# Two linear scans of a hybrid transformer block on one core: 64-token chunks in two passes, or centred 128-token chunks with the states first

## The chip, the core and the metric

The kernel runs on one core of a Trainium2 chip. A core has a matrix engine (TensorE, PE), a vector engine (VectorE, DVE), an activation engine (ScalarE, ACT), a general-purpose engine (GpSimd, POOL) and an engine that issues most transfers here (SyncE, SP). Each takes its instructions in the order in which they were laid down and waits on semaphores. Matmuls read SBUF and write PSUM, which has eight banks of 128 partitions x 512 fp32 values. The metric is device time in microseconds, the median over runs.

## The reference

Two layers work on 256 context tokens and 1024 latent tokens of width 1024. Each layer normalises and modulates its input, projects it (`w_in`), feeds four mixers (a convolution, a gated linear attention, a softmax attention and a retention), projects their outputs and adds an MLP. The second layer needs no outputs for the context. The part that is changed is the linear scan of the gated attention and of the retention, four heads each, keys of 32 and values of 64, forward and backward:

```
b = cumsum(log_a within a chunk)
q_dec = q * exp(b);  k_inv = k * exp(-b);  k_end = k * exp(b_last - b)
scores = where(lower_tri, q_dec @ k_inv.T, 0);  o_intra = scores @ v
kv = k_end.T @ v;  S = exp(b_last) * S + kv      # chunk after chunk
o = o_intra + q_dec @ S_before
```

Context and latents are one sequence of 1280 tokens; backward, the context is scanned first too. The two directions' outputs are added, normalised per head (`rms_norm`), scaled and gated. In the gated attention the decay `log_a` differs per token and key channel and comes from a small projection `z`; in the retention it is one constant per head, and queries and keys of the latents are rotated.

## The kernel before

The tokens stand in three blocks, `t` = 0, 1, 2, of 256, 512 and 512 tokens, or ten tiles `i` of 128. All large products are exact to nearly fp32 by splitting both sides in a high and a low part (`whi`/`wlo`, `ahi`/`alo`) and summing three matmuls of reduced fp32 (`mm3`); `colA` gives channels x tokens, `tokB` tokens x channels. Small products are fp32, and a trace shows each as two passes.

A layer goes through stages: convolution inputs and gates, attention operands, the gated attention's projection (`gla_in`), the retention's (`ret_in`, with the end of the convolution, `conv_tail`, beside it), then the mixers, the output projection and the MLP. Between projection and mixers the operands go through DRAM (`glaraw`, `retraw`, `attraw`).

*Projection.* `gla_in` projects one tile with two `tokB` of 264 columns. From `z` it makes `la`, the log of the decay (`gab`), with one matmul and four elementwise steps, four cumulated sums with the 64-token matrices `tri`, their exponentials (`gex`), and six products (`gpre`). `ret_in` projects 512 columns and rotates token-major.

*Mixers.* Pass 1 (`gla1`, `ret1`) loads a tile, forms outer products of keys and values, steps the forward state, transposes queries and keys, spreads the queries over four heads (`gqef`, `gqeb`, `rqe`), forms scores, masks them, and makes forward outputs and the backward direction's inner part. Then `gla_states` and `ret_states` run the backward states, and pass 2 (`gla2`, `ret2`) adds the backward state's part and finishes a tile (`finish`: norm, two transposes, gate). A gated tile is two chunks of 64 tokens, a retention tile one of 128.

The attention runs beside this, one step of `attend` for each step of the scans, in three streams: `prep` (transposes of queries and keys into a bank, from there two ScalarE copies `ka`, and `kb`, `qa`), `rowmax` (scores of a tile against all keys, three segments of 512, 512 and 256, each reduced by VectorE), and `main` (scores `sb`, exponential `aP`, weights times values `ob`, running sums). The two heads of a `main` step write the two halves of one bank `ob`. What is left of it when the scans end runs alone.

PSUM in the mixers: `sb` 2 banks, `ob` 1, `mb` 1, `pb` 1, `gb` 2, `rb` 1. `prep` uses `pb`, and `rowmax` alternates:

```
b = bank(("mb", "pb")[(h_ + j) % 2])
```

The order on each engine is that of a scheduling layer, which starts from the program's order and moves instructions past each other by its own estimates; the tables of order below show what came out.

Of the kernel before, what the change touches and what calls it, by code (L numbers as in the profile page):

```python
# [8 lines left out]
F32 = mybir.dt.float32  # L9
# [22 lines left out]
def _consts():  # L32
# [3 lines left out]
    same = (p[:, None] // 64) == (p[None, :] // 64)  # L36
    s, t = p[:, None], p[None, :]
    sl, tl = (p % 64)[:, None], np.arange(64)[None, :]
    parts["maskfb"] = np.concatenate([(sl <= tl) * 1.0, (sl >= tl) * 1.0], axis=1)
    parts["tri"] = np.concatenate(  # L40
        [(same & (s <= t)) / 16.0, (same & (s > t)) / 16.0, (same & (s >= t)) / 16.0, (same & (s < t)) / 16.0], axis=1)
    parts["ind"] = np.stack([(p < 64) / 16.0, (p >= 64) / 16.0], axis=1)
    lg = np.log1p(-np.exp2(-5.0 - np.arange(4)))
# [4 lines left out]
    blk = (p[:, None] // 32 == np.arange(4)[None, :]) * 1.0  # L48
    parts["blk"] = blk * sc
    parts["retqf"] = (blk[:, :, None] * np.exp((t + 1) * hp)[:, None, :]).reshape(128, 512)  # L50
    parts["retqb"] = (blk[:, :, None] * np.exp((128 - t) * hp)[:, None, :]).reshape(128, 512)
# [3 lines left out]
    for nm, hd in (("ret", 32), ("att", 64)):  # L55
        n = hd // 4
        inv = 10000.0 ** (-np.arange(n) / n)
        ang = np.concatenate([(tok // 64)[..., None] * inv, (tok % 64)[..., None] * inv], axis=-1)
        parts["cos" + nm] = np.cos(ang).reshape(128, -1)
        parts["sin" + nm] = np.sin(ang).reshape(128, -1)  # L60
# [33 lines left out]
def build(tc, a, out, dbg=None):  # L94
# [41 lines left out]
    retraw = dram.tile([NTILE, 128, 512], F32, name="retraw")  # L136
    glaraw = dram.tile([NTILE, 128, 1024], F32, name="glaraw")
# [222 lines left out]
    # ------------------------------------------------------------------ start  # L360
# [53 lines left out]
    for l in range(2):  # L414
# [3 lines left out]
        # -------------------------------------------------------- in projections  # L418
# [15 lines left out]

        def raw():
            return ag.tile([128, 528], F32, tag="rst", name="rst", bufs=5)
# [82 lines left out]
        # attention operands: rms norm and rotation, token-major  # L519
# [70 lines left out]
        # gated linear attention operands: decays, decayed queries and keys  # L590
        ag = pools.get("ag", bufs=2)
        tri = ag.tile([128, 512], F32, name="tri", bufs=1)
        ind = ag.tile([128, 2], F32, name="ind", bufs=1)
        nc.sync.dma_start(out=tri, in_=cslice("tri"))
        nc.sync.dma_start(out=ind, in_=cslice("ind"))
        sl = granule(l, [(C_GLA, 512), (C_GLAZ, 16)], 528)

        def gla_in(i):
            need_o = not (last and i < CT)
            st = raw()  # L600
            b = tokB(sl, 264, 264, i)
            nc.scalar.copy(st[:, 264:528], b[:, 0:264])
            b = tokB(sl, 0, 264, i)
            nc.scalar.copy(st[:, 0:264], b[:, 0:264])
            q, k, z = st[:, 0:128], st[:, 128:256], st[:, 512:528]
            nc.sync.dma_start(out=glaraw[i, :, 768:1024], in_=st[:, 256:512])
            zt = ag.tile([17, 128], F32, tag="zt", name="zt")
            nc.gpsimd.memset(zt, 1.0)
            yield
            b = bank(f"c{i % 2}")  # L610
            tr(b[0:16, 256:384], z)
# [3 lines left out]
            ab = ag.tile([128, 256], F32, tag="gab", name="gab")  # L615
            nc.scalar.activation(ab, b[:, 0:256], AF.Abs)
            act(ab, ab, AF.Exp, "exp", scale=-1.0)
            act(ab, ab, AF.Ln, "exp", bias=1.0)
            la = ab
            nc.vector.scalar_tensor_tensor(la, b[:, 0:256], 0.0, ab, op0=ALU.min, op1=ALU.subtract)  # L620
# [4 lines left out]
            b = bank(f"c{i % 2}")  # L625
            for j in range(4):
                mm(b[:, j * 128:(j + 1) * 128], tri[:, j * 128:(j + 1) * 128], la[:, (j // 2) * 128:(j // 2) * 128 + 128], True, True)
            yield
            pre = ag.tile([128, 6, 128], F32, tag="gpre", name="gpre")
            ex = ag.tile([128, 4, 128], F32, tag="gex", name="gex")  # L630
            act(ex.rearrange("p a b -> p (a b)"), b, AF.Exp, "exp")
            if need_o:
                act(pre[:, 2:4, :], b.rearrange("p (a b) -> p a b", a=4)[:, 0:4:2, :], AF.Exp, "exp", scale=-1.0)
            yield
            kb_ = k[:, None, :].to_broadcast([128, 2, 128])
            nc.vector.tensor_tensor(pre[:, 4:6, :], ex[:, 1:4:2, :], kb_, op=ALU.mult)
            if need_o:
                nc.vector.tensor_tensor(pre[:, 0:2, :], ex[:, 0:4:2, :], q[:, None, :].to_broadcast([128, 2, 128]), op=ALU.mult)
                nc.vector.tensor_tensor(pre[:, 2:4, :], pre[:, 2:4, :], kb_, op=ALU.mult)
            x0 = 0 if need_o else 512  # L640
            nc.sync.dma_start(out=glaraw[i, :, x0:768], in_=pre.rearrange("p a b -> p (a b)")[:, x0:768])

        for _ in stagger((gla_in(i) for i in range(NTILE)), 1):
            step(taps, 3)
            step(mg)
        drain(taps)
        pools.close("ag")
        open_xy()

        ar = pools.get("ar", side="right", bufs=2)  # L650
        cosr = ar.tile([128, 8, 16], F32, name="cosr", bufs=1)
        sinr = ar.tile([128, 8, 16], F32, name="sinr", bufs=1)
        nc.sync.dma_start(out=cosr.rearrange("p a b -> p (a b)"), in_=cslice("cosret"))
        nc.sync.dma_start(out=sinr.rearrange("p a b -> p (a b)"), in_=cslice("sinret"))
        sl = granule(l, [(C_RET, 512)], 512)
        pw = load_slab(a["conv_w_pw"][l].rearrange("(k p) n -> p k n", p=128), 2, 256)
        y = [None if last and t == 0 else xy_tile(t, "y") for t in range(3)]

        def ret_in(i):
            st = ar.tile([128, 512], F32, tag="rst", name="rst")  # L660
            c0 = 128 if last and i < CT else 0
            b = tokB(sl, c0, 512 - c0, i)
            nc.scalar.copy(st[:, c0:512], b[:, 0:512 - c0])
            yield
            if i >= CT:
                t1 = ar.tile([128, 16, 16], F32, tag="rt1", name="rt1", bufs=1)
                t2 = ar.tile([128, 16, 16], F32, tag="rt2", name="rt2", bufs=1)
                x3 = st[:, 0:256].rearrange("p (h d) -> p h d", d=16)
                j = i - CT
                nc.gpsimd.tensor_tensor(t2, x3, sinr[:, j:j + 1, :].to_broadcast([128, 16, 16]), op=ALU.mult)  # L670
# [576 lines left out]
```

## Time and profile before

| | |
|---|---|
| median of 3 runs | 3361.87 us (3356.07 to 3367.40) |
| span of the profiled execution | 3332.9 us |
| its own time outside the span | not recorded; the median is 29.0 us above the span |
| PE busy | 3248.3 us (97%), 17209 matmul passes |
| DVE, ACT, POOL busy | 1762.8, 920.1, 245.8 us |
| granted clock, mean | 0.962 (1 is 2.4 GHz, 0.50 is 1.2 GHz) |
| gated projection, layer 0 | 268 to 352 us |
| retention projection, layer 0 | 352 to 425.5 us |
| mixers, layer 0 | 425.5 to 776 us |
| mixers, layer 1 | 2139.2 to 2500 us |

Busy time of PE counts a matmul until its modelled end, so neighbours overlap; how far apart two matmuls start says more than how long one takes. The clock is listed for each stretch. L numbers are lines of the kernel before; all matmuls have the helper's line L166, transposes L163.

### The profile page before, as it was taken

What the parts mean: (1) busy time and instruction counts of PE and PEld (TensorE: products, weight loads), DVE (VectorE), ACT (ScalarE), POOL (GpSimd) and SP (SyncE); (2) the same over time, 40 slices, a digit from 0 to 9 for tenths busy, and PEclk for the clock granted to TensorE, in tenths of its full rate; (3) what the DMA queues carried; (4) which work ended last, traced back from release to release, by engine and by line L of the source; (5) the groups of instructions that cost most, each with busy time, mean ns of one, the idle gap of its engine ahead of it and who ended that gap; (6) DMA issues with size and microseconds to landing.
All of it is one profiled execution on the core that took longest, in us unless ns stands there. A gap on an engine that the chain in (4) does not pass through costs nothing. (4 is left out here: it accounts for less than half of the span.)

```text
span 3332.9 us, 42190 instructions
## 1 busy us (share of the span) xinstructions
PE 3248.3 (97%) x17209; PEld 2475.9 (74%) x17209; DVE 1762.8 (53%) x3026; ACT 920.1 (28%) x1839; POOL 245.8 (7%) x255
## 2 busy tenths in 40 slices
PE   7999989999999999999999999899999999999999
PEld 5778856556888888888888779666557788888887
DVE  4683344676554444454446892235674644444545
ACT  4123432334322111111113334322243311111222
POOL 0011110331000000000000020201340000000000
PEclk8999997999999999999999999858899999999999
DMA  8354131003122222211111222210003111111111
GB/s 277 94 161 133 62 109 35 14 17 117 37 91 83 89 83 76 89 51 39 39 38 59 87 82 79 73 60 29 4 29 120 57 40 43 51 51 51 51 38 51
DMA packets 206523, 232.26 MB, mean 70 GB/s; under 512 B 19714, under 2 KB 160728, under 8 KB 206328
## 3 DMA queue, kind: packets, MB, share of 16 engines
q1 hardware_dynamic: 205592, 227.84, 21.4%
q8 instruction: 135, 2.21, 0.3%
q0 software_dynamic: 736, 1.72, 0.2%
q14 instruction: 60, 0.49, 0.0%
HBM read 191.11 MB, written 38.40 MB: 69 GB/s over the span
## 5 line engine op out<-in xcount | busy, mean ns | idle before, releaser
L166 PE MATMUL bank<-ahi,whi 128*128 128x512 f32 (+1 forms) x1920 | 720.0, 375 | 13.5 <-ACT tmp L153 6.6
L166 PE MATMUL bank<-ahi,wlo 128*128 128x512 f32 (+1 forms) x1920 | 720.5, 375 | 0.0
L166 PE MATMUL bank<-alo,whi 128*128 128x512 f32 (+1 forms) x1920 | 719.6, 375 | 0.9 <-DVE alo L357 0.9
L1156 DVE SCALAR_TENSOR_TENSOR x<-bank,mods,x 128x512 f32<-128x512 f32 (+1 forms) x640 | 438.5, 694 | 260.7 <-PE bank L166 259.0
L166 PE MATMUL bank<-hh,whi 128*128 128x512 f32 (+1 forms) x1280 | 475.9, 372 | 0.0
L166 PE MATMUL bank<-hl,whi 128*128 128x512 f32 (+1 forms) x1280 | 475.3, 371 | 0.0
L166 PE MATMUL bank<-hh,wlo 128*128 128x512 f32 (+1 forms) x1280 | 473.9, 370 | 0.0
L166 PEld LDWEIGHTS bank<-ahi,whi 128*128 128x128 f32 x1920 | 364.8, 190 | 100.5 <-DVE x L1156 8.2
L166 PEld LDWEIGHTS bank<-alo,whi 128*128 128x128 f32 x1920 | 362.9, 189 | 73.3 <-DVE alo L357 2.0
L166 PEld LDWEIGHTS bank<-ahi,wlo 128*128 128x128 f32 x1920 | 362.2, 189 | 67.8 <-issue 2.1
L160 DVE TENSOR_TENSOR wlo<-wst,whi 128x1024 fp32r<-128x1024 f32 (+1 forms) x186 | 224.9, 1223 | 269.1 <-ACT whi L159 268.9
L159 ACT CAST whi<-wst 128x1024 fp32r<-128x1024 f32 (+1 forms) x186 | 191.6, 1044 | 621.6 <-PE bank L166 473.1
L166 PEld LDWEIGHTS bank<-hh,whi 128*128 128x128 f32 x1280 | 240.5, 188 | 45.6
L166 PEld LDWEIGHTS bank<-hh,wlo 128*128 128x128 f32 x1280 | 239.9, 187 | 46.5 <-issue 0.2
L166 PEld LDWEIGHTS bank<-hl,whi 128*128 128x128 f32 x1280 | 240.4, 188 | 43.9 <-issue 0.2
L1140 ACT ACTIVATE tmp<-bank 128x512 f32<-128x512 f32 (+1 forms) x160 | 88.4, 553 | 658.5 <-PE bank L166 657.4
L1142 DVE TENSOR_TENSOR tmp<-tmp 128x512 f32<-128x512 f32 (+1 forms) x160 | 102.0, 639 | 308.5 <-ACT hh L1141 306.7
L166 PE MATMUL bank<-whi,ahi 128*128 128x512 f32 (+3 forms) x640 | 220.1, 346 | 8.3 <-ACT whi L159 8.3
L166 PE MATMUL bank<-wlo,ahi 128*128 128x512 f32 (+3 forms) x640 | 219.9, 344 | 4.2 <-DVE wlo L160 4.2
L166 PE MATMUL bank<-whi,alo 128*128 128x512 f32 (+3 forms) x640 | 216.6, 339 | 0.0
L463 DVE SCALAR_TENSOR_TENSOR yacc<-u,wdw,yacc 128x1295 f32<-128x1295 f32 (+1 forms) x120 | 166.4, 1432 | 0.3
L166 PEld LDWEIGHTS bank<-whi,ahi 128*128 128x128 f32 x640 | 122.0, 191 | 30.1 <-issue 9.2
(240 smaller groups left out, 3731.2 us busy)
## 6 DMA issues: line engine op xcount, KB each, us to landing
wm<-in_w_mod_dram SPq DMA_DIRECT2D x96, 512.0 KB, 4.1
wst<-in_w_up_dram SPq DMA_DIRECT2D x64, 512.0 KB, 4.2
wst<-in_w_down_dram SPq DMA_DIRECT2D x64, 512.0 KB, 3.5
wst<-in_w_in_dram SPq DMA_DIRECT2D x32, 512.0 KB, 4.6
graw<-glaraw SPq DMA_DIRECT2D x18, 512.0 KB, 3.4
wst<-in_w_out_dram SPq DMA_DIRECT2D x16, 512.0 KB, 4.0
x<-xdram SPq DMA_DIRECT2D x4, 2048.0 KB
glaraw<-gpre SPq DMA_DIRECT2D x18, 384.0 KB, 2.3
```

The costliest lines, as they stand in the source:

```text
L159: nc.scalar.copy(hi, src)
L160: nc.vector.tensor_tensor(lo, src, hi.bitcast(F32), op=ALU.subtract)
L166: nc.tensor.matmul(ps, lhsT=lhsT, rhs=rhs, start=start, stop=stop)
L463: nc.vector.scalar_tensor_tensor(yv, uv, wv, yv, op0=ALU.mult, op1=ALU.add)
L1140: nc.scalar.activation(rl[:, :n], b[:, :n], AF.Relu)
L1142: nc.vector.tensor_tensor(rl[:, :n], rl[:, :n], rl[:, :n], op=ALU.mult)
L1156: nc.vector.scalar_tensor_tensor(xt[t][:, d, :], b[:, :n], mod(l, 5, d, seg), xt[t][:, d, :], op0=ALU.mult, op1=ALU.add)
```

## The change

The gated scan's chunk grows from 64 to 128 tokens. The cumulated decay is centred on the middle of the chunk, so that one sum gives the factor of the queries, `exp(e)`, and of the keys, `exp(-e)`; what is missing at the ends comes from `gdec`, two decays per half chunk.

The projection stage now works block by block. Values and `z` are projected token-major (272 or 256 columns), keys and queries channel-major with `colA`. Factors are applied there, the retention's rotation is a matmul with a matrix `rot`, and the queries are stored twice, with the odd or the even heads set to zero (`msk`). Each tile's end-of-chunk keys are transposed and multiplied with the values (`outer`); these products go to DRAM (`glakv`, `retkv`) with the factors (`glaf`, `retf`) and the values.

The mixers first run all states of both directions (`states`) and then each block's tiles without any dependence between them (`scan_tile`), gated first, then the retention, and finish a whole block at once with a matmul against a block matrix in place of transposes (`scan_block`). Scores are formed for two heads at a time on one half of the rows, each half into its own bank. PSUM in the mixers is now `sb` 2, `ob` 1, `mb` 1, `sc` 2, `oo` 2; `pb` is gone, and `prep` and `rowmax` both use `mb`. The convolution's output goes through DRAM (`yconv`), and the mixers' output tiles are opened later.

```diff
-    parts["maskfb"] = ...
-        [(same & (s <= t)) / 16.0, (same & (s > t)) / 16.0, (same & (s >= t)) / 16.0, (same & (s < t)) / 16.0], axis=1)
+        [1.0 * (s <= t) - (s <= 63), 1.0 * (s >= t) - (s >= 64)], axis=1) / 16.0
...
+        def outer(kd, v, i, pool, dst):
+            bk = bank()
+            for d_ in range(2):
+                for h_ in range(4):
+                    mm(bk[hs(h_), d_ * 64:(d_ + 1) * 64], kd[:, d_, hs(h_)], v[:, h_ * 64:(h_ + 1) * 64], True, True)
+            kv = pool.tile([128, 128], F32, tag="kvt", name="kvt")
+            nc.scalar.copy(kv, bk[:, 0:128])
+            nc.sync.dma_start(out=dst[i], in_=kv)
...
+        def gla_fac(t):
+            bk = colA(sl, 128, t)
+            if need_o:
+                bq = colA(sl, 0, t)
...
+            for d_ in range(2):
+                e = ebank[t][d_]
+                ex = ag.tile([128, 2, 512], F32, tag="gex", name="gex", bufs=1)
+                act(ex[:, 0, :n], e[:, :n], AF.Exp, "exp", scale=-1.0)
+                nc.vector.tensor_tensor(gk[:, d_, :n], bk[:, :n], ex[:, 0, :n], op=ALU.mult)
+                if need_o:
+                    act(ex[:, 1, :n], e[:, :n], AF.Exp, "exp")
+                    for j in range(2):
+                        nc.vector.scalar_tensor_tensor(gq[:, 2 * d_ + j, :n], bq[:, :n], msk[:, j:j + 1], ex[:, 1, :n],
+                                                       op0=ALU.mult, op1=ALU.mult)
...
+            for i in tiles_of(t):
+                ke = ag.tile([128, 2, 128], F32, tag="ke", name="ke", bufs=1)
+                for d_ in range(2):
+                    nc.scalar.mul(ke[:, d_, :], gk[:, d_, c0:c0 + 128], gdec[:, i, d_, 1 - d_:2 - d_])
+                b = bank()
+                for d_ in range(2):
+                    tr(b[:, d_ * 128:(d_ + 1) * 128], ke[:, d_, :])
+                kt = ag.tile([128, 2, 128], F32, tag="ket", name="ket")
+                nc.vector.tensor_copy(kt, b[:, 0:256].rearrange("p (a b) -> p a b", a=2))
+                outer(kt, gst.pop(i), i, ag, glakv)
+
+        def gla_block(t):
+            yield from stagger((gla_in(i) for i in tiles_of(t)), 1)
+            yield from gla_fac(t)
...
+        def ret_block(t):
...
+                    mm(br[:, :n], rc["rot"], x[:, :n], True, True)
+                    nc.vector.tensor_tensor(t2[:, :n], br[:, :n], cs[:, 1, :], op=ALU.mult)
+                    nc.vector.tensor_tensor(x[:, :n], x[:, :n], cs[:, 0, :], op=ALU.mult)
+                    nc.vector.tensor_tensor(x2[:, :n], x[:, :n], t2[:, :n], op=ALU.add)
...
+                    for d_ in range(2):
+                        for j in range(2):
+                            nc.vector.scalar_tensor_tensor(rq[:, 2 * d_ + j, :n] ...
...
-        open_psum("psa", sb=2, ob=1, mb=1, pb=1)
-        open_psum("psm", gb0=1, gb1=1, rb=1)
+        open_psum("psa", sb=2, ob=1, mb=1)
+        def bank2(tag):
+            return psm.tile([128, 2, 512], F32, tag=tag, name=tag, bufs=1)
...
+            kvs[nm] = mp.tile([128, NTILE, 2, 64], F32, name=nm + "kv", bufs=1)
+            nc.sync.dma_start(out=kvs[nm].rearrange("p i d c -> p i (d c)"), in_=src.rearrange("i p c -> p i c"))
...
+        def scan_tile(kind, i, obk):
...
+            sc = bank2("sc")
+            for d_ in range(2 if kind == "g" else 1):
+                for p in range(2):
+                    rows = slice(64 * p, 64 * p + 64)
+                    mm(sc[:, p, d_ * 256:(d_ + 1) * 256], x[rows, 4 + d_, :],
+                       x[rows, 2 * d_:2 * d_ + 2, :].rearrange("p a b -> p (a b)"), True, True)
...
+            for h_ in range(4):
+                mm(obk[64 * (h_ % 2):64 * (h_ % 2) + 64, h_ // 2, c0:c0 + 128], v[:, h_ * 64:(h_ + 1) * 64], ab[:, h_, :], True, False)
+            for m_, (d_, s_) in enumerate(inter):
+                for j in range(2):
+                    for p in range(2):
+                        mm(obk[64 * j:64 * j + 64, p, c0:c0 + 128], s_[rows, :], x[rows, 2 * d_ + j, :], False, m_ == len(inter) - 1)
...
+        def scan_block(kind, t):
+            obk = bank2("oo")
+            yield from stagger((scan_tile(kind, i, obk) for i in tiles_of(t)), 1)
+            nc.scalar.copy(os_[:, :, :n], obk[:, :, :n])
+            nc.scalar.activation(sq[:, :, :n], os_[:, :, :n], AF.Square)
+            sc = bank2("sc")
+            for p in range(2):
+                mm(sc[:, p, :n], mc["blk64"], sq[:, p, :n], True, True)
+            act(sq[:, :, :n], sc[:, :, :n], AF.Ln, "exp", bias=eps, scale=1.0 / 64)
+            act(sq[:, :, :n], sq[:, :, :n], AF.Exp, "exp", scale=-0.5)
...
-                    b = bank(("mb", "pb")[(h_ + j) % 2])
+                    b = bank("mb")
...
-        for _ in pass1:
-            step(aa_)
-        pools.close("m1")
-        ret_states()
-        gla_states()
-        for _ in pass2:
+        for _ in scans():
             step(aa_)
```

How the instructions stand on the engines, at three places. First PE in the gated projection of layer 0, before: the rows around the cumulated sums of one tile, with dense matmuls of the next tile (`bank<-w..,a..`) on both sides.

```order
L166 MATMUL bank<-whi,alo_546 128x264
L166 MATMUL c_2468<-ind,gab 128x2 x2
L166 MATMUL c_2557<-wa_83,zt 128x256
L166 MATMUL bank<-whi,ahi_545 128x264
L166 MATMUL c_2630<-gab,tri 128x128 x4
L166 MATMUL bank<-wlo,ahi_545 128x264
```

The same place with the change: the end of block 1, after the last dense matmul of its queries (`colA`), to the first of block 2.

```order
L177 MATMUL bank<-ahi_513,wlo 128x512
L174 MATMUL bank<-ident,ke 128x128 x2
L177 MATMUL bank<-rst,ket 32x64 x8
L174 MATMUL bank<-ident,ke 128x128 x2
L177 MATMUL bank<-rst,ket 32x64 x8
L174 MATMUL bank<-ident,ke 128x128 x2
L177 MATMUL bank<-rst,ket 32x64 x8
L174 MATMUL bank<-ident,ke 128x128 x2
L177 MATMUL bank<-rst,ket 32x64 x8
L177 MATMUL bank<-whi,ahi_550 128x272
```

The transposes of `ke` and the outer products (`rst,ket`) of four tiles stand in a row, with no dense matmul between them.

Second, PE in a step of the attention's `main` in layer 0, before. The `ob` row is the product of both heads.

```order
L166 MATMUL pb<-ka,qa 128x512
L166 MATMUL pb<-kb,qa 128x512
L166 MATMUL mb<-ka,qa 128x512
L166 MATMUL mb<-kb,qa 128x512
L166 MATMUL sb<-qa,ka 128x512
L166 MATMUL sb<-tmp,kb 128x512
L166 MATMUL sb<-qa,ka 128x512
L166 MATMUL sb<-tmp,kb 128x512
L166 MATMUL ob<-aP,ve 64x512 x2
```

And with the change, the same matmuls of a step.

```order
L177 MATMUL sb<-qa,ka 128x512
L177 MATMUL sb<-tmp,kb 128x512
L177 MATMUL sb<-qa,ka 128x512
L177 MATMUL sb<-tmp,kb 128x512
L177 MATMUL mb<-ka,qa 128x512
L177 MATMUL mb<-kb,qa 128x512
L177 MATMUL ob<-aP,ve 64x512
L177 MATMUL mb<-ka,qa 128x256
L177 MATMUL mb<-kb,qa 128x256
L177 MATMUL ob<-aP,ve 64x512
```

Both row-maximum segments write `mb`, and the second stands between the two heads' `ob`.

Third, SP at the start of the mixers of layer 0, before: the last stores of the retention's projection, the first loads of the scans (`graw`, `rraw`) and of the attention (`arw`, `ve`).

```order
L675 DMA retraw<-rst 128x512 x8
L949 DMA ve<-attraw 128x64 x3
L675 DMA retraw<-rst 128x512
L771 DMA graw<-glaraw 128x1024
L858 DMA rraw<-retraw 128x512
L948 DMA arw<-attraw 128x192 x4
```

With the change (`retkv` are the outer products, `rkv` all of them loaded back, `y` the convolution's output).

```order
L613 DMA retkv<-kvt 128x128
L934 DMA ve<-attraw 128x64 x4
L808 DMA y_3922<-yconv 128x2x256
L808 DMA y_3923<-yconv 128x2x512
L829 DMA rkv<-retkv 128x10x128
L933 DMA arw<-attraw 128x192 x4
```

The first `arw` loads stand behind the load of all outer products, which reads what the store just above writes.

## Rows read from the trace of the kernel before

**Rows 1.** From the page: the span, and busy time of each engine.

```profile
span 3332.9 us, 42190 instructions
PE 3248.3 (97%) x17209; PEld 2475.9 (74%) x17209; DVE 1762.8 (53%) x3026; ACT 920.1 (28%) x1839; POOL 245.8 (7%) x255
```

**Rows 2.** Windows: stretch, its length, busy PE, PEld, DVE, ACT, POOL; clock.

```profile
268.00:352.00 84.00, 82.69 (x627) 76.15 (x628) 23.61 (x52) 32.96 (x84) 4.12 (x12) 0.96 0.39 127
...
425.50:571.00 145.50, 134.35 (x1121) 85.74 (x1121) 65.40 (x177) 41.40 (x148) 16.76 (x21) 0.84 0.26 79
571.00:776.00 205.00, 204.65 (x1071) 110.81 (x1071) 136.97 (x340) 75.35 (x181) 66.77 (x56) 0.98 0.06 18
2139.20:2300.00 160.80, 148.03 (x1013) 92.39 (x1013) 57.51 (x155) 37.84 (x131) 12.74 (x17) 0.64 0.23 70
2300.00:2500.00 200.00, 199.76 (x976) 103.12 (x975) 136.29 (x308) 73.29 (x166) 69.41 (x57) 0.94 0.05 16
```

**Rows 3.** Windows of tile `gb`, then `rb`: PE, PEld, DVE, ACT; clock.

```profile
571.00:776.00 205.00, 32.48 (x358) 24.72 (x358) 14.02 (x37) 4.02 (x13) 0.98 0.06 18
2300.00:2500.00 200.00, 26.45 (x290) 19.64 (x290) 10.84 (x29) 2.52 (x8) 0.94 0.05 16
...
571.00:776.00 205.00, 25.15 (x180) 19.41 (x180) 13.04 (x35) 2.41 (x9) 0.98 0.06 18
2300.00:2500.00 200.00, 21.15 (x152) 16.10 (x152) 11.39 (x30) 2.04 (x8) 0.94 0.05 16
```

**Rows 4.** Timeline of PE: start us, length us, operation, passes; one head, both heads.

```profile
573.69 1.07 PE L166 MATMUL ob<-aP,ve 128*64 128x512 f32 x2
...
586.35 1.08 PE L166 MATMUL ob<-aP,ve 128*64 128x512 f32 x4
```

**Rows 5.** Timeline of PE: an outer product and a score product, and what follows.

```profile
584.43 0.43 PE L166 MATMUL rb<-rraw,rkd 128*32 128x64 f32 x16
584.79 0.50 PE L166 MATMUL pb<-kb,qa 64*128 64x512 f32 x1
...
591.28 0.60 PE L166 MATMUL gb<-gqef,gkt 128*64 128x256 f32 x4
591.71 0.60 PE L166 MATMUL gb<-gqeb,gkt 128*64 128x256 f32 x4
```

**Rows 6.** Lines by form: count | busy us, mean ns | idle before.

```profile
L153 ACT ACTIVATE aP<-sb 128x512 f32<-128x512 f32 x160 | 88.8, 595 | 142.2 <-PE sb L166 141.6
...
L972 DVE TENSOR_REDUCE amx<-mb 128x1 f32<-128x512 f32 x64 | 43.9, 685 | 42.2 <-PE mb L166 42.1
...
L166 PE MATMUL mb<-ka,qa 128*128 128x512 f32 x64 | 34.2, 534 | 0.0
...
L1113 DVE SCALAR_TENSOR_TENSOR x<-bank,mods,x 128x512 f32<-128x512 f32 x32 | 23.9, 748 | 63.6 <-PE bank L166 61.3 <-DMA x<-xdram 2.3
...
L166 PE MATMUL c<-gab,tri 128*128 128x128 f32 x160 | 21.2, 275 | 0.0
...
L834 DVE SCALAR_TENSOR_TENSOR gkv<-gkv,gdec 128x64 f32<-128x64 f32 x36 | 12.7, 354 | 1.0 <-ACT gkv L788 0.4
```

**Rows 7.** Timeline of one preparation and the next one's transposes.

```profile
455.15 0.49 PE L163 MATMUL pb<-ident,arw 128*64 128x128 f32 x3
...
455.68 0.26 ACT L956 CAST ka<-pb 64x128 fp32r<-64x128 f32 x1
...
456.95 0.42 DVE L962 TENSOR_TENSOR qa<-pb,qa 64x256 fp32r<-64x256 f32 x1
...
458.76 0.49 PE L163 MATMUL pb<-ident,arw 128*64 128x128 f32 x3
```

**Rows 8.** Windows around an idle PE, columns as in Rows 2.

```profile
264.60:268.00 3.40, 0.12 (x2) 0.12 (x1) 1.88 (x5) 1.24 (x2) 1.86 (x2) 1.00 0.37 119
268.00:274.80 6.80, 6.01 (x26) 5.71 (x27) 4.55 (x14) 2.59 (x8) 2.23 (x2) 0.50 0.84 266
```

**Rows 9.** From the page: a load from DRAM, KB, us from issue to landing.

```profile
graw<-glaraw SPq DMA_DIRECT2D x18, 512.0 KB, 3.4
```

More of the change, by code (lines that the diff above doesn't have):

```diff
@@ L647, in build @@
         pools.close("ag")
[L648 to L654, printed above, removed]
+        ar = pools.get("ar", bufs=2)
+        rc = {}
+        for nm in ("rot", "rdec", "retkd", "msk"):
+            rc[nm] = ar.tile([128, OFF[nm][1]], F32, name="r_" + nm, bufs=1)
+            nc.sync.dma_start(out=rc[nm], in_=cslice(nm))
@@ L655, in build @@
         sl = granule(l, [(C_RET, 512)], 512)
         pw = load_slab(a["conv_w_pw"][l].rearrange("(k p) n -> p k n", p=128), 2, 256)
[L657 to L670, printed above, removed]
-                nc.vector.tensor_tensor(t1, x3, cosr[:, j:j + 1, :].to_broadcast([128, 16, 16]), op=ALU.mult)
-                yield
-                nc.vector.tensor_tensor(x3[:, 0:16:2, :], t1[:, 0:16:2, :], t2[:, 1:16:2, :], op=ALU.subtract)
-                nc.vector.tensor_tensor(x3[:, 1:16:2, :], t1[:, 1:16:2, :], t2[:, 0:16:2, :], op=ALU.add)
-            nc.sync.dma_start(out=retraw[i, :, c0:512], in_=st[:, c0:512])
@@ L706, in build @@
         pools.close("ar", "convp", "actp", "wp", "psd")
-        open_psum("psa", sb=2, ob=1, mb=1, pb=1)
-        open_psum("psm", gb0=1, gb1=1, rb=1)
+        open_xy()
+        y = [None if last and t == 0 else xy_tile(t, "y") for t in range(3)]
+        for t in tts:
+            o, n = TOK[t]
+            nc.sync.dma_start(out=y[t][:, 0:2, :], in_=yconv[:, :, o:o + n])
+        open_psum("psa", sb=2, ob=1, mb=1)
+        psm = pools.get("psm", space=PS)
+        def bank2(tag):
+            return psm.tile([128, 2, 512], F32, tag=tag, name=tag, bufs=1)
@@ L746, in finish @@
             else:
[L747 removed]
+                nc.vector.tensor_tensor(ab4, s0, mc["retm"].rearrange("p (a b c) -> p a b c", a=2, b=2), op=ALU.mult)
             yield
[L749 to L752 removed]
@@ L904, in ret_states @@
-        def ret_states():
-            for n_, i in enumerate(back[1:-1]):
-                nc.vector.scalar_tensor_tensor(rkv[:, i, :], rkv[:, back[n_], :], mc["retdec"], rkv[:, i, :], op0=ALU.mult, op1=ALU.add)
-        def ret2(i):
-            if last and i < CT:
-                return
-            n_ = back.index(i)
-            bo = None
-            if n_ > 0:
-                bo = bank("rb")
-                qe = mp.tile([128, 4, 128], F32, tag="rqe2", name="rqe2")
-                nc.gpsimd.tensor_tensor(qe, rq[:, i, :][:, None, :].to_broadcast([128, 4, 128]),
-                                        mc["retqb"].rearrange("p (h c) -> p h c", h=4), op=ALU.mult)
-                for h_ in range(4):
-                    mm(bo[:, h_ * 64:(h_ + 1) * 64], qe[:, h_, :], rkv[:, back[n_ - 1], :], True, True)
-            yield
-            yield from finish("rb", None if n_ == 0 else bo[:, 0:256], n_ == 0, i, "ret_norm_g", 2, 6)
@@ L923, in both, with scans @@
-        def both(*gens):
-            live = list(gens)
-            while live:
-                live = [g_ for g_ in live if next(g_, par) is not par]
-                if live:
-                    yield
-        pass1 = both(stagger((gla1(i) for i in range(NTILE)), 3), stagger((ret1(i) for i in range(NTILE)), 3))
-        pass2 = both(stagger((gla2(i) for i in back), 4), stagger((ret2(i) for i in back), 4))
+        def scans():
+            yield from states()
+            for kind in ("g", "r"):
+                for t in tts:
+                    yield from scan_block(kind, t)
```

405 lines of the change are left out of this document (178 added, 227 removed).

## The prediction

> **What bounds the kernel now.** I read the page first, then the busy time by stretches, then the timeline of single matmuls. The page says that TensorE (PE) is busy for 97% of the span [rows 1], so a change pays by taking PE time away or costs by making PE wait. The table by stretches [rows 2] shows where the change falls. From 268 to 425.5 (first layer) the recurrences' projections run; in the gated one, to 352, PE is at work for 82.7 of 84.0 us. From 425.5 to 776, and from 2139.2 to 2500 in the second layer, attention and scans run together. I cut each at its first `ob` matmul (weights times values): a **first part** of 145.5 and 160.8 us, and a **second part** of 205.0 and 200.0 us, in which PE is busy for all but 0.6 us. VectorE and ScalarE have room in all of them (137 of 205 us at most). The clock is the other thing to see: 0.84 and 0.64 in the first parts, near 1 in the second.
>
> **The change part by part.** All sums are against the profiled execution, whose span is 3332.9 us [rows 1]. The median of the three timed runs is 29.0 us above that span, and I add it at the end.
>
> *Second part.* The scans' matmuls (`gb`, `rb`) take 32.5 + 25.2 = 57.6 us there, and 26.5 + 21.2 = 47.6 in the second layer [rows 3]. Their tails overlap their neighbours, so I take nine tenths: 52 and 43 us go. What comes in is the retention scan. Four passes of 256 columns on two column halves take 0.43 us, 591.28 to 591.71 [rows 5]. So the two score matmuls of a retention tile take 0.43, the four with values about 0.5, the eight with states 0.43, and for the switches between shapes I allow 0.45, which no row separates: 1.8 us a tile, 2.2 for a gated tile with its four score matmuls. The norms' block sums are matmuls of 512 columns at 1.0 (below). That is 10 x 1.8 + 5 = 23 us in the first layer, 8 x 1.8 + 4 = 18 in the second.
>
> Nothing before shows two matmuls on different *row* halves at once, which the new scores and state products need. Bounds: the column price if rows behave like columns, double if not. I take the first, since its row has the same size and passes; the other end is 0.86 + 0.43 more for a gated tile and 0.43 + 0.43 for a retention tile, 39 us over 36 tiles. The Trainium skill (TensorEngine Tiling (Array Packing), Key Properties) says that row tiles run independently too, which would keep the sum as it is; no row here shows it.
>
> Row maxima lose a bank. `mb` and `pb` alternated; now there is only `mb`, and in the new order a row-maximum pair, or an `sb` pair, stands between the two heads' `ob` matmuls. The two together take 1.08 us (586.35), one alone 1.07 (573.69) [rows 4]: apart, a pair costs 1.0 us more. In the order 8 and 2 pairs were apart, now 30 and 30: +22 and +28 us. In exchange the `ob` between two row maxima covers most of the reduction (0.685 us [rows 6]); I leave 5 us a layer for what it doesn't. Second part: -52 + 23 + 22 + 5 = -2, and -43 + 18 + 28 + 5 = +8. Sum **+6 us**.
>
> *First part.* The gated scan's PE work shrinks to 10 x 2.2 + 5 = 27 us, but it is no longer what the part waits for. All 20 attention preparations and 26 row-maximum segments (18 of 512 keys, 8 of 256) now pass one after another through the bank `mb`. A preparation holds its bank from the transposes at 455.15 to the end of the last VectorE subtraction at 456.95 + 0.42, 2.2 us; the next transposes came 3.6 us after the first [rows 7]. Ends 2.2 and 3.6; I take 2.75, nearer to the lower, since between them stands less scan work than before. 20 x 2.75 = 55 us. A segment of 512 keys is two matmuls of 0.53, the second starting while the first drains, and the reduction: about 1.7 us [rows 6]. With VectorE's scan products in the way I take 2.1, and 1.45 for 256 keys: 18 x 2.1 + 8 x 1.45 = 49 us. Ahead stands a new chain: on SP's queue the load `rkv<-retkv` waits for the last outer product's write, and the first `arw` loads are queued behind it. Two transfers at up to 3.4 us [rows 9] and ten state updates at 0.354 [rows 6] before the first `kb`, partly side by side: 9.5 us. Together 9.5 + 55 + 49 = 114 us for 145.5 and 160.8: -31.5 and -47, sum **-78 us**.
>
> *Projections.* Two of four `tri` matmuls a tile go, half of 21.2 us over both layers [rows 6]: 5 us less a layer. The dense work keeps its columns in a fifth fewer instructions, which I put at another 5. But the outer products now end each block, and in the order nothing dense stands between them. After the last dense matmul of a gated block of 512 tokens VectorE makes two `gq` (2 x 0.748), ScalarE one exponential (0.595), VectorE `gk` (0.75) and two more `gq` (1.5) [rows 6], then the first `ket` copy (0.42): 4.8 us before the first outer product. Each of the four tiles then takes transposes 0.33, copy 0.42, outer product 0.36 (584.43 to 584.79 [rows 5]) and hand-overs, 1.45 in a row with PE waiting in each: 9.6 us. The block of 256 takes 5.3 likewise, the last one 11, since weight splits and norm steps stand between on VectorE: 26 us a layer. The decay chain of a block's last tiles, formerly under 48 dense matmuls, is under ten: 6 us. Gated: 26 + 6 - 10 = 22, and 21 in the second layer, whose first block needs no queries.
>
> Retention: four rotations at 1.0 us, each behind a ScalarE copy of 0.6 with its hand-overs, 7 us; block ends at 4, 5.5 (conv work covers part) and 9 us, where four `rq` products at 0.748 precede most key products on VectorE; dense 1 less: 24.5 us. ScalarE, POOL and the stores lie beside this and cost nothing; POOL only loses query products.
>
> The clock: after the idle 3.4 us at 264.6 the next 6.8 us ran at 0.50 [rows 8], a loss of 3.4. Four of a layer's six block ends leave PE as idle: 14 us. A rule speaks against the change here. The Trainium skill (TensorE: Matmul & The Clock Gate, Why this matters for your kernels) warns of gaps between bursts, which put the array back to the low level. By it all six ends would pay, 6.8 us a layer more than my sum; the trace agrees for the gap at 264.6.
>
> Projections: 22 + 24.5 + 14 = 60.5, and 59.5. Sum **+120 us**.
>
> Total: 120 - 78 + 6 = +48, a span of 3381 and a time of **3410 us**.
>
> **The rivals.** *Faster: PE's work sets the pace of the first part, not the bank.* Scan matmuls fill each wait for the bank, and the part takes the start (9.5), transposes 20 x 0.49, row maxima 26 x 0.75, scans 27 and small things 3: 69 us, 45 less a layer. 3410 - 90 = 3320. For it speaks that PE was at work for 134 of 145.5 us before [rows 2]; against it that the 46 uses of the bank leave some 50 us of waiting (20 x 1.7, 18 x 0.75, 8 x 0.45) for 27 of scan work, on an engine that takes its matmuls in order. It decides from 90 us a first part downwards: there the whole change is even. Chance 0.20.
>
> *Even: the block ends cost half.* If exponentials and products of a block are done before its last dense matmul more often than I see, and the clock holds, 120 becomes 70: 3360. Against it: `gq` needs the very last dense sum. Chance 0.13.
>
> *Much slower: preparations keep their present step.* At 3.6 us each and 2.5 a segment the first part is 145 us a layer, 31 more: 3472. For it speaks the step before [rows 7], against it that half of that step was scan work which is gone. Chance 0.17. The serial row halves (+39, part of it under waits) fall into the same region.
>
> **How the numbers follow.** My forecast has 0.50. Its own range, with first parts of 100 to 128 us and block ends give or take a quarter, is 3355 to 3455. The whole range, to the faster case and the slower one: 3330 to 3480. This measurement tells no difference under about 0.3%, 10 us: 3352 to 3372. Faster: 0.20 and a quarter of the even case, 0.23. No change: 0.07 of the even case and 0.05 from the forecast's lower end, 0.12. Slower: the rest, 0.65.
>
> **What would show it.** Right: in the first parts PE idle for a third, waiting for VectorE on `mb` and `sc`, over 100 us long; in the second parts PE full, about 200 us; PE gaps after each block of the gated projection, and outer products some 1.4 us apart; low clock behind them. Wrong: first parts under 90 us, or outer products close behind the dense work. Score matmuls 0.2 us apart rather than pairs with equal starts would say that row halves don't overlap.

## The result and the profile after

The changed kernel takes 3412.7 us (median of four runs) beside 3359.0 for the kernel before: a ratio of 1.0137 with the 95% interval 1.0094 to 1.018, 54 us slower. The forecast was 3410, its range 3330 to 3480. Run again later beside other runs of the kernel before, it gave 3423.1 and 1.0205 (1.0163 to 1.0247).

Two rows of the page answer to [rows 1].

```profile
span 3413.0 us, 39626 instructions
PE 3226.0 (95%) x16109; PEld 2384.8 (70%) x16109; DVE 1714.9 (50%) x2821; ACT 898.0 (26%) x1640; POOL 165.4 (5%) x178
```

TensorE (PE) is at work 22 us less, and the span is 80.1 us longer. The profiled run of the changed kernel took 3414.8, only 1.8 above its span. So the 29 us that the forecast added to the span were no time around it: the one profiled execution of before lay that far below the timed ones. The 45 later runs of the kernel before bear this out. Each took 1.7 or 1.8 us more than its span, and their times follow the mean granted clock, from 3383 us at 0.945 to 3321 at 0.967; those at the profiled execution's 0.962 took 3333 to 3335. In spans the forecast was 3381 and missed by 32; by medians, +48 was forecast and +54 measured. The place of the miss can be read, because the two traces can be laid side by side. Windows of the kernel before, cut where the stages end: projections, the mixers to the first `ob`, and from there to the output projection, each for both layers. Columns as in [rows 2].

```profile
268.00:425.50 157.50, 155.20 (x976) 134.16 (x976) 47.48 (x111) 66.45 (x153) 17.17 (x25) 0.98 0.28 93
2003.40:2139.20 135.80, 132.84 (x835) 115.92 (x833) 32.81 (x77) 55.09 (x131) 12.24 (x20) 1.00 0.16 58
425.50:573.70 148.20, 137.05 (x1132) 86.96 (x1132) 66.00 (x178) 42.79 (x151) 17.37 (x22) 0.84 0.26 78
2139.20:2309.20 170.00, 157.23 (x1064) 97.15 (x1064) 62.93 (x171) 41.32 (x139) 13.55 (x19) 0.66 0.22 67
573.70:795.90 222.20, 218.51 (x1122) 115.75 (x1121) 152.34 (x358) 88.91 (x208) 74.03 (x61) 0.98 0.11 33
2309.20:2503.80 194.60, 190.56 (x925) 98.36 (x925) 134.14 (x297) 73.61 (x164) 68.59 (x56) 0.94 0.06 20
```

The same stages of the changed kernel.

```profile
268.00:484.70 216.70, 187.40 (x1342) 152.14 (x1342) 64.93 (x140) 75.19 (x183) 12.92 (x22) 0.88 0.32 102
2049.00:2240.70 191.70, 168.93 (x1196) 137.02 (x1196) 48.13 (x102) 64.21 (x160) 8.42 (x18) 0.87 0.23 74
484.70:618.00 133.30, 96.14 (x442) 48.13 (x442) 57.02 (x149) 27.87 (x75) 0.61 (x1) 0.65 0.32 94
2240.70:2371.70 131.00, 95.92 (x431) 47.27 (x427) 55.92 (x144) 28.60 (x72) 1.88 (x2) 0.63 0.32 90
618.00:841.50 223.50, 220.20 (x875) 94.26 (x874) 121.09 (x250) 83.38 (x144) 51.40 (x43) 0.98 0.13 38
2371.70:2584.80 213.10, 205.87 (x716) 82.75 (x715) 104.50 (x207) 70.18 (x115) 47.28 (x38) 0.92 0.10 31
```

Projections: +59.2 and +55.9 (forecast +60.5 and +59.5). Mixers, both parts together: 370.4 to 356.8 and 364.6 to 344.1, so -13.6 and -20.5 (forecast -33.5 and -39). Two things are to be seen in the middle rows: PE is at work for only 96 of 133 us, and at 0.65 of its clock.

A block end of the gated projection, on PE's timeline (start, length, what ended the idle time before).

```profile
332.03 0.39 PE L177 MATMUL bank<-ahi,wlo 128*128 128x512 f32 x1
...
335.86 0.48 PE L174 MATMUL bank<-ident,ke 128*128 128x128 f32 x1 [3.33 <-ACT ke L681]
337.07 0.66 PE L177 MATMUL bank<-rst,ket 128*32 128x64 f32 x16 [0.74 <-DVE ket L687]
...
338.87 0.65 PE L177 MATMUL bank<-rst,ket 128*32 128x64 f32 x16 [0.52 <-DVE ket L687]
...
342.45 0.66 PE L177 MATMUL bank<-rst,ket 128*32 128x64 f32 x16 [0.52 <-DVE ket L687]
343.04 0.60 PE L177 MATMUL bank<-whi,ahi 128*128 128x272 f32 x1
```

The first outer product comes 5.0 us after the last dense matmul (forecast 4.8), the next ones 1.79 apart (1.45), the block end takes 11.0 (9.6). From 334.8 to 348.5 the granted clock was 0.50. The four preparations at the mixers' start:

```profile
498.52 0.82 PE L174 MATMUL mb<-ident,arw 128*64 128x128 f32 x3 [13.83 <-DMA arw<-attraw]
501.60 0.82 PE L174 MATMUL mb<-ident,arw 128*64 128x128 f32 x3 [2.26 <-issue]
504.25 0.82 PE L174 MATMUL mb<-ident,arw 128*64 128x128 f32 x3 [1.83 <-issue]
505.00 2.07 PE L177 MATMUL sc<-gx 64*128 64x256 f32 x6
507.01 0.85 PE L174 MATMUL mb<-ident,arw 128*64 128x128 f32 x3
```

The start waits 13.8 us (9.5 forecast), the first steps are 3.1, 2.7 and 2.8 (2.75), and three transposes take 0.82 us at a granted clock of 0.50, for the 0.49 of [rows 7] at 1.00. In the second part, `ob` as a pair, then apart, and the two score matmuls of a retention tile:

```profile
692.56 1.08 PE L177 MATMUL ob<-aP,ve 128*64 128x512 f32 x4
...
694.39 0.70 PE L177 MATMUL sc<-rx 64*128 64x256 f32 x4
695.02 0.50 PE L177 MATMUL mb<-ka,qa 128*128 128x512 f32 x1
...
697.00 1.07 PE L177 MATMUL ob<-aP,ve 128*64 128x512 f32 x2
698.00 0.50 PE L177 MATMUL mb<-ka,qa 128*128 128x512 f32 x1
698.43 0.50 PE L177 MATMUL mb<-kb,qa 64*128 64x512 f32 x1
698.86 0.64 PE L177 MATMUL ob<-aP,ve 128*64 128x512 f32 x1
```

A pair takes 1.08, a lone head 1.07, as in [rows 4]. The two scores on two row halves pass in 0.63 us with the switch of shape; one after the other the passes alone would take 0.86 (twice the 0.43 of [rows 5]). The eight passes of a gated tile, with no switch among them, show it at full clock (shortest, median and longest in ns; first and last start):

```profile
L177 PE MATMUL sc<-gx x8: 376/376/480, 523.2 to 523.9; 64*128 64x256 f32 x8
```

They start within 0.8 us. One after the other, at half of 0.43 each, the last would start 1.5 us after the first. Row halves overlap.

### The profile page after: what moved, and what is told of

Read it like the earlier page. It is cut to its first block, busy times and chain, and to the rows that moved or that the text cites. A ratio compares the mean times of both kernels' runs of the same rounds, so it can differ in the third digit from the quotient of the medians.

```text
span 3413.0 us, 39626 instructions
## 1 busy us (share of the span) xinstructions
PE 3226.0 (95%) x16109; PEld 2384.8 (70%) x16109; DVE 1714.9 (50%) x2821; ACT 898.0 (26%) x1640; POOL 165.4 (5%) x178
## 5 line engine op out<-in xcount | busy, mean ns | idle before, releaser
L177 PE MATMUL bank<-ahi,whi 128*128 128x512 f32 (+1 forms) x2096 | 785.8, 375 | 12.2 <-ACT tmp L164 6.6
L177 PE MATMUL bank<-alo,whi 128*128 128x512 f32 (+1 forms) x2096 | 785.3, 375 | 0.9 <-DVE alo L368 0.9
L177 PE MATMUL bank<-ahi,wlo 128*128 128x512 f32 (+1 forms) x2096 | 785.4, 375 | 0.0
L177 PEld LDWEIGHTS bank<-ahi,whi 128*128 128x128 f32 x2096 | 398.4, 190 | 104.7 <-DVE x L1136 8.2
L177 PEld LDWEIGHTS bank<-alo,whi 128*128 128x128 f32 x2096 | 396.1, 189 | 79.4 <-issue 4.0
L177 PEld LDWEIGHTS bank<-ahi,wlo 128*128 128x128 f32 x2096 | 395.7, 189 | 74.0 <-issue 3.8
L177 PEld LDWEIGHTS bank<-hh,wlo 128*128 128x128 f32 x1280 | 239.9, 187 | 46.5 <-issue 0.2
L957 DVE TENSOR_REDUCE amx<-mb 128x1 f32<-128x512 f32 (+1 forms) x200 | 118.8, 594 | 197.6 <-PE mb L177 196.0
L177 PE MATMUL bank<-whi,ahi 128*128 128x256 f32 (+2 forms) x480 | 162.3, 340 | 8.8 <-ACT whi L170 8.8
L177 PE MATMUL bank<-wlo,ahi 128*128 128x256 f32 (+2 forms) x480 | 160.5, 335 | 6.0 <-DVE wlo L171 6.0
L177 PE MATMUL bank<-whi,alo 128*128 128x256 f32 (+2 forms) x480 | 158.5, 330 | 0.0
```

The costliest lines, as they stand in the source:

```text
L177: nc.tensor.matmul(ps, lhsT=lhsT, rhs=rhs, start=start, stop=stop)
L957: nc.vector.reduce_max(mx[:, j:j + 1], b[:, :kn], axis=AX.X)
```

## Experiments

Ratios are to the kernel before, run beside each group. "First part" includes the start gap.

**Block ends under the next block's dense work.**

```
             nc.sync.dma_start(out=glaf[:, 4:6, o:o + n], in_=gk[:, :, :n])
-            for i in tiles_of(t):        # ke, ket, outer
+            tails.append(gla_tail(t, gk))
...
 for _ in par((map(gla_block, range(3)), 1)):
+    tail(3)
```

(the retention blocks likewise; the last gated end lies in the first retention block, so the retention's tiles move into the gated projection's pool)

> The ends of the blocks (ke and key-decay products, their transposes, the outer products) are issued among the next block's dense matmuls, two rounds late; the gated projection's last end lies in the first retention block. Same computation. Theory (block ends are the cost of the projections): PE's idle time there falls from 30 of 217 us to under 12 in the first layer and likewise in the second, the granted clock there rises from 0.88 to 0.95 or more, each layer's projections shorten by 25 to 35 us, the time by 45 to 75: about 3350. Rival (the projections are longer because the dense work itself takes longer in its new shape and order): the idle time goes, the dense matmuls do not get faster, under 20 us in all: about 3395.

Measured: 3374.4 us, ratio 1.0081 (1.0054 to 1.0108). The projections, both layers:

```profile
268.00:451.00 183.00, 172.48 (x1342) 144.11 (x1341) 64.99 (x137) 72.75 (x179) 13.06 (x22) 0.96 0.36 114
2022.00:2185.70 163.70, 155.51 (x1196) 130.29 (x1196) 49.13 (x103) 61.61 (x159) 8.43 (x18) 0.95 0.27 87
```

They fall by 33.7 and 28.0 us; idle time from 29.3 to 10.5 in the first layer, clock from 0.88 to 0.96: the theory, and the prediction's term. The whole gained a little less than expected: 38 us by medians, 40 by spans, and by the ratios 0.6% of the changed kernel's first group of runs and 1.2% of its second. The mixers behind grew by 6.5 and 14.8 us; how far two executions of one kernel differ there is shown below, under *The changed kernel again*.

**The start chain.**

```
-rw = at_.tile([128, 3, 64], F32, tag="arw", name="arw", bufs=4)
+rw = pre.tile([128, 3, 64], F32, tag="arw", name="arw", bufs=4)   # a pool of its own
...
-yield from states()
+yield from states("g")
...
+if (kind, t) == ("g", 1): yield from states("r")    # with the load rkv<-retkv
```

> The attention rows (arw) get space of their own, so that their first loads are issued before the last outer products, and the retention states with their load come behind the first gated block. Same computation. Theory (the 13.8 and 11.4 us in which PE waits at the mixers' start are a serial chain of loads): the two gaps fall to 3 to 4 us each, the low clock behind them gets shorter, time 15 to 25 us less: about 3392. Rival (the preparations behind it are paced by their bank and by VectorE, so that what is gained at the start is lost to waits in the next 40 us): 5 us less or nothing.

Measured: 3396.5, ratio 1.0152 (1.0101 to 1.0202), not told from the changed kernel, whose two ratios are 1.0137 and 1.0205. By medians it is 16 us less, as the theory has it, by spans 8, by the first of those ratios nothing. The gaps fell from 13.8 and 11.4 to 3.7 and 3.2 us, also the theory, but the first parts only went from 133.3 and 131.0 to 130.5 and 132.2. That looks like the rival, that what waits behind the start takes the gain back. Yet the part behind the start ran at a granted clock of 0.59 and 0.62, for 0.67 and 0.64, and the unedited kernel, run again (below), was about as long there at that lower clock: 128.7 and 123.9 us, for 126.8 and 129.1 here. What the edit is worth alone stays open.

**Preparations in the score banks.**

```
-                b = bank("mb")          # prep
+                b = bank("sb")
...
-                    b = bank("mb")      # rowmax
+                    b = bank(tag)       # "sb" for head 1 of the first block, else "mb"
```

> The preparations, and the second head's maxima of the first token block, use the two banks of the scores, which stand empty in the first part. Same computation. Theory (46 uses of the single bank pace the first part): the step from one preparation to the next falls from 3 us to under 2.4, the first parts from 133 and 132 us to 108 to 118, time 28 to 45 us less: about 3376. Rival (the first part is long because TensorE runs it at 0.6 to 0.7 of its clock, with 85 per cent of the time busy, and not for the bank): under 12 us less: about 3404.

Measured: 3367.5, ratio 1.0047 (1.0012 to 1.0082), some 0.9% better than the changed kernel in its first group of runs, 1.6% better than in its second. The two first parts without their start:

```profile
494.00:571.80 77.80, 73.02 (x198) 35.07 (x198) 40.61 (x117) 24.07 (x71) 1.88 (x2) 0.50 0.31 90
2231.90:2319.40 87.50, 80.25 (x269) 38.51 (x269) 41.70 (x115) 23.50 (x66) 1.10 (x1) 0.54 0.31 88
```

They were 119.5 and 119.6: the single bank did pace them. Much of the scans moved behind the first `ob`, so the mixers as a whole gained 13.9 and 24.0. Now look at the clock: 0.50 and 0.54, in the first layer with PE at work for 73 of 77.8 us. That raised the next question.

**Value products in pairs.**

```
+    if "mb" in maxs_:                       # main, ob of head 0
+        after_(i_, maxs_["mb"])
+    tc.add_manual_dep(i_, ex_[j].name, ...)
...
+    if "ob" in maxs_:                       # rowmax
+        after_(i_, maxs_["ob"])
```

(`ex_[j]` is head 1's exponential, so that both products become ready together; `maxs_` holds the last row maximum and the last `ob` of head 1, so that neither passes the other)

> Both heads' products with the values stand next to each other in all 84 pairs; row maxima keep one bank and come before or after a pair in the order in which they are written. Same computation. Theory (a pair apart costs 1.0 us more, 58 pairs a layer are cut in the first kernel's order of instructions): the ob time falls from 66 to 46 us in the second parts, these from 223 and 213 us to about 200 and 192, time 35 to 45 us less: about 3373. Rival (the product between two maxima covers their reduction on VectorE; side by side the maxima wait for it instead): half or all of it comes back as waits for the bank, 0 to 15 us less: about 3405.

Measured: 3386.7, ratio 1.0128 (1.0076 to 1.0181); span 3379.2. Windows of the tile `ob` alone (PE, PEld, DVE): the second parts of the kernel before, of the changed kernel, and of this one.

```profile
573.70:795.90 222.20, 53.76 (x176) 10.51 (x176) 3.60 (x6) 0.98 0.11 33
2309.20:2503.80 194.60, 47.75 (x160) 8.73 (x160) 2.73 (x4) 0.94 0.06 20
```

```profile
618.00:841.50 223.50, 77.25 (x176) 14.49 (x176) 3.59 (x6) 0.98 0.13 38
2371.70:2584.80 213.10, 78.78 (x160) 13.98 (x160) 2.73 (x4) 0.92 0.10 31
```

```profile
623.40:818.20 194.80, 46.87 (x176) 9.10 (x176) 3.61 (x6) 0.99 0.15 44
2362.90:2549.40 186.50, 47.43 (x160) 8.43 (x160) 2.73 (x4) 0.92 0.12 36
```

`ob` falls by 30 and 31 us and the second parts by 28.7 and 26.6, but the first parts grow by 8.3 and 14.5: by spans the change is -34, by the ratios alone it stays unclear. (The 58 cut pairs that the expectation gives to a layer are those of both layers.) Leaving the pairs out of the four edits (below) settles it.

**The changed kernel again.** No edit.

> The changed kernel itself, unaltered, beside the runs that follow. All theories: the same as before, 3400 to 3420 us, ratio to the kernel before 1.01 to 1.02.

Measured: 3423.1, ratio 1.0205 (1.0163 to 1.0247); a little above the expectation. Its profiled execution has a span of 3423.9 us, 10.9 longer than the first. The two first parts:

```profile
482.90:625.50 142.60, 106.91 (x446) 52.58 (x442) 57.15 (x149) 27.81 (x75) 0.61 (x1) 0.58 0.30 88
2247.50:2382.90 135.40, 99.27 (x429) 48.60 (x427) 55.85 (x144) 28.54 (x72) 1.87 (x2) 0.61 0.31 88
```

They were 133.3 and 131.0 us, at 0.65 and 0.63 of the clock: 9.3 and 4.4 us lie between two executions of the same kernel. Without their start they take 128.7 and 123.9 us at 0.59 and 0.62. So differences of that size in a first part, in the single edits above, say nothing about the edit.

**All four edits.**

> The four edits together: block ends under the next block's dense matmuls, own space for the first attention rows, preparations in the score banks, pairs of value products side by side. Same computation. Theory (the four terms lie in different stages; with the single bank gone the start chain counts too): the savings seen one at a time add up, -40 -20 -43 -33 on the profiled span of 3413, less a part for the half clock of the first parts: 3280 to 3315. Rival (each edit only moves the same wait or the same half clock along, as the gain at the start was lost again in the first part): no more than the best single one, 3350 or above.

Measured: **3220.1**, ratio **0.9601** (0.9562 to 0.964): 4% faster than the kernel before and better than the theory. The single edits moved the span by -40, -8, -43 and -34, together -125; the four together by -194. Against the span of the changed kernel's second execution these are -168 and -205, so the four gain some 37 to 69 us more than their sum. The mixers fell to 287.6 and 280.4 us.

**Filler.** On the kernel with preparations in the score banks:

```
+fb = bank("ob")                      # empty before the first main
+filler(24)                           # 128x512 matmuls of constants into fb
...
     tr(...)                          # prep's transposes
+    filler(2)
```

> The kernel with preparations in the score banks, and added to it work that nothing uses: 24 matmuls of 128x512 on an unused bank at the mixers' start and two behind each of the 20 preparations of a layer. Result unchanged. Its base ran both first parts at 0.50 of the clock, 78 and 88 us with PE at work for 93 per cent. Theory (the low level is entered in the idle start and held because the preparations' and scans' small matmuls do not raise it): with the filler the granted clock of the first parts rises above 0.85, they get shorter by 20 to 30 us each in spite of 64 more matmuls, time 30 to 50 us below its base: about 3325. Rival (the level does not depend on it, or PE's clock does not pace the part): the first parts get longer by the filler's own 9 to 17 us each, time 10 to 30 us above the base: about 3387.

Measured: 3314.2, ratio 0.9882 (0.9839 to 0.9926), 53 us below its base, by work that nothing uses. Its first parts without the start:

```profile
496.00:552.10 56.10, 53.83 (x241) 29.20 (x241) 40.06 (x118) 23.46 (x71) 1.11 (x2) 0.97 0.43 125
2198.80:2266.30 67.50, 63.60 (x305) 34.20 (x305) 40.31 (x116) 21.50 (x64) 0.61 (x1) 0.87 0.40 114
```

The clock rose from 0.50 and 0.54 to 0.97 and 0.87, and the parts fell from 77.8 and 87.5 to 56.1 and 67.5.

**Filler on the four edits.**

> The four edits together, with the filler matmuls of the run before. Result unchanged. Theory (half clock in the first parts is what is left): 25 to 45 us below the four edits alone, 3245 to 3285. Rival (filler is only work): 10 to 30 us above them.

Measured: 3232.2, ratio 0.9641 (0.9589 to 0.9693), no gain. The first parts without their start ran at 1.00 and 0.87 and took 64.4 and 76.3 us for 76.4 and 82.8, but the 24 fillers stood ahead of the first preparation and brought the start gap back to 13.3 and 12.0 us.

**Filler on the changed kernel as it is.**

> The changed kernel with its single bank for maxima and preparations, and the filler: 24 matmuls of 128x512 at the mixers' start, two behind each preparation, nothing uses them. Result unchanged. Theory (half clock is what made the first parts longer than forecast): their granted clock rises from 0.67 and 0.64 to over 0.85, and they fall from 133 and 132 us, the start included, to 108 to 120, near the forecast's 114; time 25 to 50 us less than the changed kernel: about 3382. Rival (the single bank paces them whatever the clock, and filler is work in its chain): 10 us less at most, or up to 20 more: about 3425.

Measured: 3423.3, ratio 1.0197 (1.0155 to 1.0239), as without it.

```profile
495.40:614.70 119.30, 100.31 (x489) 52.64 (x489) 53.90 (x135) 28.31 (x75) 0.61 (x1) 0.76 0.29 83
2257.10:2379.30 122.20, 106.82 (x441) 54.73 (x441) 50.30 (x127) 28.45 (x71) 0.63 (x2) 0.68 0.25 72
```

The rival: the clock rose only to 0.76 and 0.68, and the parts kept their 119 and 122 us. Behind one bank PE still waits for 19 us of 119.

**Filler on the kernel before.**

> The kernel before, with the same filler matmuls and nothing else changed. Result unchanged. Theory (half clock costs the kernel before as well, its first parts ran at 0.84 and 0.64): the second layer's first part gets shorter by 20 to 35 us, the first layer's by 0 to 10, less the filler's own work: time 10 to 35 us below the kernel before, ratio 0.990 to 0.997. Rival (the clock follows the scan's small matmuls, of which the kernel before has three times as many, and filler behind the preparations is too little to change it): 10 to 30 us above, ratio 1.003 to 1.009.

Measured: 3322.6, ratio 0.9906 (0.9874 to 0.9938). Behind the start its first parts rose from 0.85 and 0.66 of the clock to 0.94 and 0.77; start included, they fell from 148.2 and 170.0 us to 143.1 and 149.5: the theory.

**The four edits without one of them.**

> The four edits without the pairs of value products: block ends, start, score banks only. Same computation. Theory (a cut pair costs 1.0 us wherever it is): 40 to 55 us above the four edits, about 3267. Rival (the gain above the sum of the single edits, some 70 us, comes from the pairs' order, which also keeps the first part's small matmuls apart): 70 us or more above, 3290 or more.

Measured: 3273.9, ratio 0.9753 (0.9718 to 0.9787): the pairs are worth 54 us there, the theory.

> The four edits without the start chain's: arw shares its space and the retention states come first, as in the changed kernel. Same computation. Theory (with the single bank gone the start gap stands in series, and the low clock that it brings stays): 20 to 45 us above the four edits, about 3250. Rival (the gap is made up later, as when the edit was made alone): within 8 us of the four edits.

Measured: 3278.0, ratio 0.9767 (0.9731 to 0.9804): the start chain, which alone was not told from nothing, is worth 58 us beside the other three, more than the 20 to 45 of the theory; 37 of them lie in the first parts. The first parts without their start, then those of the four edits:

```profile
469.60:553.40 83.80, 78.91 (x234) 38.91 (x234) 42.39 (x122) 24.55 (x72) 1.88 (x2) 0.50 0.31 90
2155.00:2246.50 91.50, 86.38 (x262) 40.04 (x262) 43.69 (x123) 24.46 (x67) 0.61 (x1) 0.50 0.26 76
```

```profile
456.00:532.40 76.40, 68.46 (x330) 36.10 (x330) 47.55 (x134) 25.68 (x74) 1.88 (x2) 0.74 0.53 152
2112.20:2195.00 82.80, 76.27 (x332) 38.90 (x332) 45.57 (x129) 24.40 (x67) 0.61 (x1) 0.66 0.40 111
```

With the gap (16.2 and 12.9 us) both layers' first parts run at 0.50 from end to end; without it at 0.74 and 0.66.

## Why the prediction was right, and where it was not

- **Projections, right in sum (+115 for +120), with two errors that cancel.** Idle time rose by 27 us in the first layer (29.3 against 2.3). What the clock took is (1 - 0.88) x 216.7 less (1 - 0.98) x 157.5, 23 us, and 25 in the second layer, where the forecast had 14. Hardly more block ends paid than the four of six: five in the first layer, four in the second. But the stretch at 0.50 behind one was as long as 13.7 us, where the sum had 6.8 for each, so the ends alone cost 19 us a layer. And the start of the stage ran at 0.50 too, for over 10 us in both layers, against 6.8 and none before. The Trainium skill (TensorE: Matmul & The Clock Gate, Why this matters for your kernels) warned of just these gaps; nine of the twelve ends agree. That all six of a layer would pay, as the forecast worked out by that rule, did not come true. The rest of the stage (ends, decay chain and rotations, less what the dense work saves) was dearer in my sum than in the trace (36 and 31 against 46.5 and 45.5 a layer, clock aside). Moving the ends under dense work took back 34 and 28 us.
- **Second part, right in its main term.** `ob` costs 23.5 and 31 us more by its tile's windows, 22 and 28 were forecast; the pairs put back bring 54 us in the end. As a whole the part came out at +1.3 and +18.5 us for -2 and +8; the second layer's other 10 us were not traced to a term. Row halves overlap, as the forecast took it; here the trace agrees with the Trainium skill's rule that tiles of the array are independent (TensorEngine Tiling (Array Packing), Key Properties).
- **First part, the step that failed.** "Together 9.5 + 55 + 49 = 114 us" came out as 133.3 and 131.0. That the bank paces it was right: two more banks took 42 and 32 us from the part behind the start (some of it moved behind the first `ob`; the mixers as a whole gained 13.9 and 24.0). The sizes were not. The start is 13.8 and 11.4. Behind it in the first layer, from one use of `mb` to the next, the 20 preparations took 58.6 us for 55 and the 26 row-maximum segments 60.9 for 49. The terms were priced from rows mostly at full clock, while the part runs at 0.65 and 0.63. Where the trace has full clock the prices hold: a preparation takes 2.6 us on average (2.75 in the sum) and a segment of 512 keys 1.8 (2.1). At 0.50 they take 3.1 and 3.0. The faster rival's 69 us of PE work were 96 in the trace, and 96 x 0.65 is 62. I charged the clock to the projections and never to the part behind the idle start, though [rows 2] showed 0.64 there before. Raising the clock alone does not give the difference back, though: with the filler alone the segments fell to some 57 us, but the preparations, with fillers behind each, rose to 62. Here clock and bank had to be freed together: filler alone did nothing, the bank alone left the clock at 0.50, both gave 53 us more.
- **The time came out closer than the working, by luck.** The stages missed by 33 us (mixers by 38, projections by -5). The 29 us that I took for time around the span stood in for it.
- **Open.** By the profiled pair the change costs 80 us, by the medians 54 and 66; the profiled execution of before had drawn a high clock (0.962, where the later runs' middle one had 0.957). What decides the clock that one execution gets was not tried. Nor was it told apart whether the filler works by the 24 matmuls at the start or by those behind the preparations.

## What to carry to other kernels

Work that only waits for other engines belongs between dense matmuls, not at a block's end: the gap is paid once as idle time and again as half clock behind it (moving the ends gave back 62 us here). Read the granted clock beside the busy share of each stretch, since a PE at work for 94% may be running at half its rate. And try edits to one stage together: an edit whose gain alone was lost among the runs' differences (the start) was worth 58 us beside the others. Before reading a few microseconds of a stage as an edit's work, look how far the stage moves between two executions of the same kernel.

## What the runs showed of the hardware

- A stretch of 78 us ran at 0.50 of the clock (1.2 GHz) with PE at work for 94% of it and no wait above 1.7 us; what it did was transposes, matmuls on parts of the array and those of the row maxima. In the four edits without the start, PE was at work for 31.99 of the 32.00 us from 486.4 on, and the clock was 0.50 there too. Two unused 128x512 matmuls behind each group of transposes, and 24 ahead, gave 0.97 and a shorter stretch in spite of the added work. The kernel before gained 0.9% by the same. What the clock asks for, these runs don't settle.
- The grant differs from one execution to the next, and the time with it: the same kernel before took 3321 us at a mean of 0.967 and 3383 at 0.945.
- Matmuls on the two row halves of the array overlap: the two scores of a tile passed in 0.63 us, where one after the other they would take 0.86.
